# Issuing the last six stores of a batched matrix product as three pieces each

## The chip, the cores and the metric

The kernel runs on one core of one Trainium2 chip. The metric is the device time of one execution in microseconds (us), given as the median of several runs. The profile is one execution recorded by the hardware profiler; its span runs from the first to the last instruction.

## What is computed

```python
a, b: float32, shape (1024, 64, 64)
out = np.matmul(a, b)          # 1024 products of 64 x 64 matrices, float32
```

Inputs are 16.8 MB each, and so is the output: 33.55 MB are read from HBM and 16.78 MB written.

## The kernel before

The batch is cut into 16 tiles of 64 matrices, `t` = 0 to 15 (`n_t` = 16), for `b` and for the output, and into 8 tiles of 128 matrices for `a`.

For each output tile, VectorE casts `b` to bfloat16 (`cast`), VectorE copies the transposed `a` into a block-diagonal tile (`spread`), TensorE multiplies (`multiply`, line 189), and ScalarE, with some help of VectorE, copies the product from PSUM into the tile `o_sb` in SBUF (`evacuate`, line 177). `a` was regrouped by VectorE and transposed by TensorE before that. The loop over `t` is written out by hand under a manual schedule: in each step the next tile's `spread` and `cast` come first, then the loads of tiles further ahead, then this tile's `multiply`, and then the store of the tile before it (`HOLD` = 2, so that `store(t - 1)` follows `multiply(t)`).

`o_sb` has 128 partitions of 8 KB. In the output one partition holds, for each of the eight groups of matrices `gh`, one run of 1 KB. A store of `n` groups therefore writes `n` runs of 1 KB for each partition.

Stores are made by `put(lo, n)` in `multiply`, lines 165 to 169; `lo` is the first group and `n` the number of groups. Which queue issues them is decided by `store_queue` (lines 64 to 67):

- Tiles 0 to 13 are stored whole, 1 MB in one DMA, by GpSimd's queue.
- Tile 14 is stored in two halves of 512 KB (`lo` = 0 and 4), both by the queue of SyncE (SP).
- Tile 15 is stored in four quarters of 256 KB (`lo` = 0, 2, 4, 6). Quarters 0 and 2 (`lo` = 0 and 4) are issued by ScalarE's queue (ACT) and quarters 1 and 3 by SP. ScalarE evacuates quarters 0 and 2, VectorE quarters 1 and 3.

So the last six stores are: the two halves of tile 14, called A and B below, and the four quarters of tile 15, called C (ACT), D (SP), E (ACT) and F (SP). SP issues A, B, D, F in this order, and ACT issues C, E. Nothing else is left on SP's instruction list behind F but the wait for the end (line 282, the launch), where SP waits for every completion semaphore in turn before the engines are released.

The framework gives each DMA that SP or ACT issues one of eight completion semaphores, in turn. A DMA adds 16 to its semaphore when all of it has landed. Before a semaphore is used again, the issuing queue waits until the DMA that had it before has landed. Such a wait stands in the issuing engine's instruction list, directly ahead of the DMA or in it. In this kernel the six last stores have six of the eight semaphores, and the ones that had them before were loads.

Of the kernel before, what the change touches and what calls it, by code (L numbers as in the profile page):

```python
# [13 lines left out]
def kernel(  # L14
# [19 lines left out]
    n_t, n_s = B // 64, B // 128  # L34
# [7 lines left out]
    o_v = out.rearrange("(t gh x) (mo w) n -> t (x mo) gh (w n)", gh=8, x=8, w=4)  # L42
# [21 lines left out]
    def store_queue(t, lo):  # L64
        if t < n_t - 2:
            return nc.gpsimd
        return nc.scalar if t == n_t - 1 and lo % 4 == 0 else nc.sync
# [90 lines left out]
    def multiply(t):  # L158
        at_bd = bd_tiles[t % N_BD][:].rearrange("p j g wl h mo -> p j g (wl h mo)")
        at_bd = at_bd.bitcast(bf16).rearrange("p j g (c u) -> p j g c u", u=2)  # L160
        b_bf = bbf_tiles.pop(t)
        last = t == n_t - 1
        o_sb = o_pool.tile([128, 8, 2, 2, 64], fp32, name="o_sb")

        def put(lo, n):
            store_queue(t, lo).dma_start(  # L166
                out=o_v[t, :, lo : lo + n, :],
                in_=o_sb[:, lo : lo + n].rearrange("p gh j wl n -> p (gh j wl n)"),
            )

        def evacuate(o_ps, gh, n, copies):

            for par in range(2):
                for wl in range(2):
                    src = o_ps[64 * wl : 64 * wl + 64, :, par, :, :]
                    dst = o_sb[64 * par : 64 * par + 64, gh : gh + n, :, wl, :]
                    copies[2 * par + wl](dst, src)  # L177

        for half in range(2):
            if not last:  # L180
                o_ps = o_psum.tile([128, 4, 2, 2, 64], fp32, name="o_ps")
            for g8 in range(8):
                if last and g8 % 4 == 0:
                    o_ps = t_psum.tile([128, 2, 2, 2, 64], fp32, name="at_ps")
                g = 8 * half + g8
                gl = (g8 % 4 if last else g8) // 2
                for j in range(2):
                    for u in range(2):
                        nc.tensor.matmul(  # L189
                            o_ps[:, gl, g % 2, j, :],  # L190
                            at_bd[:, j, g, :, u],
                            b_bf[:, g, 64 * u : 64 * u + 64],
                            start=(u == 0),
                            stop=(u == 1),
                        )
                if last and g8 % 4 == 3:
                    copy = nc.scalar.copy if g8 == 3 else nc.vector.tensor_copy
                    evacuate(o_ps, g // 4 * 2, 2, [copy] * 4)
            if not last:
                copies = [nc.scalar.copy] * 4  # L200
                if half and t % 2:
                    copies[2:] = [nc.vector.tensor_copy] * 2
                evacuate(o_ps, 4 * half, 4, copies)
        if last:
            held[t] = [lambda q=q: put(2 * q, 2) for q in range(4)]
        else:
            whole = t < n_t - 2
            held[t] = [lambda q=q: put(q, 8 if whole else 4) for q in ([0] if whole else [0, 4])]
# [78 lines left out]
```

## Time and profile before

| What | Value |
|---|---|
| Median of 3 runs (134.76 to 134.84) | 134.77 us |
| Span of the profiled execution | 133.1 us |
| What lies around the span, against the median | 1.7 us |
| VectorE busy | 94.5 us (71%) |
| ScalarE busy | 87.8 us (66%) |
| TensorE busy | 65.7 us (49%) |
| Moved by the DMA engines | 45.01 MB, 338 GB/s on average |

The span is that of the one recorded execution, and no time of its own is recorded beside the span; the runs' median is 1.7 us longer, and this is taken for what lies around the span. "PE" is TensorE, "DVE" VectorE, "ACT" ScalarE, "POOL" GpSimd and "SP" SyncE; a "q" behind a name (SPq, ACTq) is the engine's sequencer, which issues DMAs and waits. The core has 16 DMA engines, and all queues share them. "DMA share" is the mean busy share of the sixteen; it can go a little above 1, since neighbouring packets overlap. "Landing" is the moment at which a DMA's completion semaphore has its full count.

### The profile page before, as it was taken

The page shows a single profiled execution, that of the slowest core. Times are in us where ns is not written, and L with a number is a line of the kernel's source. Part 1 is how long each engine was busy: PE and PEld are TensorE (multiplying, and loading weights), DVE is VectorE, ACT ScalarE, POOL GpSimd, SP SyncE. Part 2 cuts the span into 40 slices and gives each one's busy share as a digit, 9 for nine tenths or more (in the row PEclk, how much of TensorE's full clock was granted, in tenths as well). Part 3 has the DMA queues.
Part 4 walks back from the last instruction along what each step waited for, and adds up shares of the span by engine and source line. Part 5 has one row for each costly group of instructions (what it writes and reads, how often), then busy time and mean ns, then how long its engine had stood idle before and what let it go on. Part 6 is the DMA issues. An engine that isn't in the chain of part 4 may idle for free.

```text
span 133.1 us, 2837 instructions
## 1 busy us (share of the span) xinstructions
PE 65.7 (49%) x1152; PEld 62.7 (47%) x1152; DVE 94.5 (71%) x120; ACT 87.8 (66%) x161; POOL 33.7 (25%) x43
## 2 busy tenths in 40 slices
PE   0005504990068386059519672986199361776000
PEld 0005304980068275058509562975199360766000
DVE  5930299208999719598999699969999994978100
ACT  3134505899128999919899759696969987099600
POOL 8981000420082072143144022203020410210000
PEclk9999999999559999968996875579756985556855
DMA  3999999999999999999999999999999999999991
GB/s 75 367 332 311 307 312 279 278 307 326 328 307 402 316 322 334 393 385 401 318 282 365 402 397 356 308 307 387 395 396 387 393 396 391 402 403 402 380 339 41
DMA packets 19021, 45.01 MB, mean 338 GB/s; under 512 B 1088, under 2 KB 3136, under 8 KB 19008
## 3 DMA queue, kind: packets, MB, share of 16 engines
q0 software_dynamic: 6832, 20.19, 50.2%
q1 hardware_dynamic: 7120, 14.68, 30.5%
q10 hardware_dynamic: 5056, 9.96, 19.8%
q8 instruction: 9, 0.15, 0.4%
q14 instruction: 4, 0.03, 0.1%
HBM read 33.55 MB, written 16.78 MB: 378 GB/s over the span
## 4 chain that ended last, share of the span: by engine, by line
DMA 54%; DVE 18%; ACT 13%; issue 4%; PE 3%; SPq 1%; DVEq 0%; ACTq 0%
DMA b_sb<-in_b_dram 54%; ACT o_sb L177 9%; DVE at_bd L133 9%; DVE b_bf L144 4%; DVE o_sb L177 3%; PE at_ps L120 2%; ACT at_sb L123 2%; ACT b_bf L144 1%; PE o_ps L189 1%; DVE a_bf L108 1%; SPq L90 1%; DVE a_bf L111 1%; ACT b_bf L151 1%; SPq L96 0%; DVEq L133 0%
## 5 line engine op out<-in xcount | busy, mean ns | idle before, releaser
L177 ACT COPY o_sb<-o_ps 64x512 f32<-64x512 f32 x106 | 61.6, 581 | 9.5 <-PE o_ps L189 8.2
L189 PEld LDWEIGHTS <-at_bd 128*128 128x128 bf16 x1024 | 42.5, 113 | 39.7 <-DVE b_bf L144 26.8
L189 PE MATMUL o_ps<-b_bf,at_bd 128*128 128x64 bf16 x960 | 41.2, 213 | 36.0 <-DVE b_bf L144 25.1
L133 DVE COPY at_bd<-at_sb 32x1024 f32<-32x1024 f32 x64 | 46.6, 728 | 13.6 <-ACT at_sb L123 11.8
L120 PE MATMUL at_ps<-identity,a_bf 128*128 128x128 f32 x128 | 22.5, 350 | 19.3 <-ACT a_bf L105 11.4
L166 POOL DMA_DIRECT2D out_dram<-o_sb x14 | 16.3, 1166 | 55.4 <-ACT at_sb L123 23.0
L120 PEld LDWEIGHTS at_ps<-identity,a_bf 128*128 128x128 f32 x128 | 20.7, 190 | 19.4 <-issue 19.4
L144 DVE CAST b_bf<-b_sb 128x2048 bf16<-128x2048 f32 x14 | 17.5, 1249 | 10.0 <-DMA b_sb<-in_b_dram 9.8
L123 ACT COPY at_sb<-at_ps 128x512 f32<-128x512 f32 x32 | 17.4, 590 | 9.9 <-PE at_ps L120 7.6
L73 POOL DMA_DIRECT2D a_sb<-in_a_dram x21 | 13.3, 650 | 27.3 <-DVE a_bf L108 20.4
L177 DVE COPY o_sb<-o_ps 64x512 f32<-64x512 f32 x14 | 9.7, 690 | 0.3
L108 DVE COPY a_bf<-a_sb 128x3072 bf16<-128x3072 bf16 x7 | 7.4, 1059 | 0.0
L105 ACT CAST a_bf<-o_sb 128x1024 bf16<-128x1024 f32 x2 | 2.1, 1044 | 5.3 <-DMA o_sb<-in_a_dram 5.3
L111 DVE CAST a_bf<-a_raw 128x1024 bf16<-128x1024 f32 x7 | 4.8, 683 | 0.0
L144 ACT CAST b_bf<-b_sb 128x2048 bf16<-128x2048 f32 x1 | 1.9, 1897 | 4.1 <-DMA b_sb<-in_b_dram 4.1
L177 DVE COPY o_sb<-at_ps 64x256 f32<-64x256 f32 x8 | 3.4, 422 | 1.3 <-PE at_ps L189 1.2
L105 DVE CAST a_bf<-o_sb 128x1024 bf16<-128x1024 f32 x2 | 2.6, 1296 | 2.4 <-DMA o_sb<-in_a_dram 2.3
L189 PE MATMUL at_ps<-b_bf,at_bd 128*128 128x64 bf16 x64 | 3.6, 242 | 1.0 <-DVE at_bd L133 1.0
L217 DVE MEMSET at_bd<- 128x4096 f32 x1 | 3.5, 3472 | 0.8 <-issue 0.8
L151 ACT CAST b_bf<-b_sb 128x512 bf16<-128x512 f32 x2 | 1.1, 615 | 4.3 <-DMA b_sb<-in_b_dram 4.3
L177 ACT COPY o_sb<-at_ps 64x256 f32<-64x256 f32 x8 | 2.9, 367 | 0.1
L214 ACT ACT_TABLE_LOAD x1 | 1.3, 1283 | 2.3 <-issue 2.3
(12 smaller groups left out, 6.1 us busy)
## 6 DMA issues: line engine op xcount, KB each, us to landing
out_dram<-o_sb POOLq DMA_DIRECT2D x14, 1024.0 KB, 22.3
a_sb<-in_a_dram POOLq DMA_DIRECT2D x21, 256.0 KB, 16.4
a_raw<-in_a_dram SPq DMA_DIRECT2D x7, 512.0 KB, 19.1
o_sb<-in_a_dram SPq DMA_DIRECT2D x2, 512.0 KB, 6.2
o_sb<-in_a_dram ACTq DMA_DIRECT2D x2, 512.0 KB, 7.3
out_dram<-o_sb SPq DMA_DIRECT2D x2, 512.0 KB, 7.4
out_dram<-o_sb SPq DMA_DIRECT2D x2, 256.0 KB, 7.7
out_dram<-o_sb ACTq DMA_DIRECT2D x2, 256.0 KB, 5.9
```

The costliest lines, as they stand in the source:

```text
L73: nc.gpsimd.dma_start(out=a_sb[:, h, :, :].rearrange("p v k -> p (v k)"), in_=a_v[s, h])
L105: copy(a_bf[:, :, h, :], a_sb[h].rearrange("p (v k) -> p v k", v=16))
L108: nc.vector.tensor_copy(a_bf[:, :, 0:3, :], cast_sb[:].rearrange("p h v k -> p v h k"))
L111: nc.vector.tensor_copy(a_bf[:, :, 3, :], raw[:])
L120: nc.tensor.transpose(at_ps[:, vo, :], a_cols[:, 4 * vo + 2 * j + wl, :], identity[:])
L123: nc.scalar.copy(at_tiles[s][:, j, :, wl, :, :], at_ps[:].rearrange("p vo (g mp) -> p g mp vo", mp=4),)
L133: nc.vector.tensor_copy(bd[rows, :, :, :, h, :].rearrange("p j g wl mo -> p j (g wl) mo"), at_tiles[t // 2][rows, :, half, :, :, :].rearrange(
L144: (nc.vector.tensor_copy if t else nc.scalar.copy)(b_bf[:], b_sb[:])
L166: store_queue(t, lo).dma_start(out=o_v[t, :, lo : lo + n, :], in_=o_sb[:, lo : lo + n].rearrange("p gh j wl n -> p (gh j wl n)"),)
L177: copies[2 * par + wl](dst, src)
L189: nc.tensor.matmul(o_ps[:, gl, g % 2, j, :], at_bd[:, j, g, :, u], b_bf[:, g, 64 * u : 64 * u + 64], start=(u == 0), stop=(u == 1),)
L217: nc.vector.memset(bd_tiles[0][:], 0.0)
```

## The change

`put` is given a second form for the last two tiles. Where it made one DMA over 128 partitions, it makes three: over partitions 0 to 111, over the next 16 - r, and over the last r. r is 1 for A, 2 for B, 5 for C, 3 for D, 7 for E and 4 for F. All three are issued by the queue that issued the whole store, one after the other. Six DMAs become eighteen: twelve on SP and six on ACT. The bytes, the engines' computing and the stores of the first 14 tiles are as they were.

```diff
         def put(lo, n):
+            if t >= n_t - 2:
+                few = (1, 2)[lo // 4] if t == n_t - 2 else (5, 3, 7, 4)[lo // 2]
+                for first, end in ((0, 112), (112, 128 - few), (128 - few, 128)):
+                    store_queue(t, lo).dma_start(
+                        out=o_v[t, first:end, lo : lo + n, :],
+                        in_=o_sb[first:end, lo : lo + n].rearrange(
+                            "p gh j wl n -> p (gh j wl n)"
+                        ),
+                    )
+                return
             store_queue(t, lo).dma_start(
                 out=o_v[t, :, lo : lo + n, :],
                 in_=o_sb[:, lo : lo + n].rearrange("p gh j wl n -> p (gh j wl n)"),
```

The pieces of a store are called by its letter and a number: A1 is A's piece of 112 partitions, A2 that of 15 and A3 that of 1.

## Prediction

> **What bounds the end now.** I read the page's chain first (section 4): it follows the loads of `b` and ends at ScalarE's last copy, so it doesn't show the stores. Then, because the change touches nothing before 120 us, I read only the last 13 us. The timeline of the tail shows when the six stores are issued:
>
> ```profile
> 119.48 2.96 ACT L177 COPY o_sb<-o_ps 64x512 f32<-64x512 f32 x5
> ...
> 120.08 5.45 SPq L166 DMA_DIRECT2D out_dram<-o_sb  x4
> 120.30 3.49 DVE L177 COPY o_sb<-at_ps 64x256 f32<-64x256 f32 x8 [1.19 <-PE at_ps L189]
> 122.46 1.89 ACT L177 COPY o_sb<-at_ps 64x256 f32<-64x256 f32 x5
> 123.99 0.40 ACTq L166 DMA_DIRECT2D out_dram<-o_sb  x1
> 124.37 1.12 ACT L177 COPY o_sb<-at_ps 64x256 f32<-64x256 f32 x3
> 125.52 0.38 ACTq L166 DMA_DIRECT2D out_dram<-o_sb  x1
> ```
>
> Computing is over at 125.5. The windows of the tail (columns: stretch, its length, busy time of PE, PEld, DVE, ACT, POOL, the granted clock, DMA share, GB/s) show what remains:
>
> ```profile
> 126.00:127.00 1.00, 0.00 (x0) 0.00 (x0) 0.00 (x0) 0.00 (x0) 0.00 (x0) 0.50 1.07 374
> 127.00:128.00 1.00, 0.00 (x0) 0.00 (x0) 0.00 (x0) 0.00 (x0) 0.00 (x0) 0.50 1.09 378
> 128.00:129.00 1.00, 0.00 (x0) 0.00 (x0) 0.00 (x0) 0.00 (x0) 0.00 (x0) 0.50 1.04 361
> 129.00:130.00 1.00, 0.00 (x0) 0.00 (x0) 0.00 (x0) 0.00 (x0) 0.00 (x0) 0.50 0.66 230
> 130.00:131.00 1.00, 0.00 (x0) 0.00 (x0) 0.00 (x0) 0.00 (x0) 0.00 (x0) 0.50 0.23 81
> 131.00:132.00 1.00, 0.00 (x0) 0.00 (x0) 0.00 (x0) 0.00 (x0) 0.00 (x0) 0.50 0.03 10
> ```
>
> The sixteen DMA engines are full until 129 and then end one by one. All is queued long before: the end is set by draining. 378 GB/s over 16 engines is 1 KB per 43 ns on each. SP's waits close it:
>
> ```profile
> SPq L282 <- DMA out_dram<-o_sb: 6.1, 1, 6.1
> SPq L166 <- DVE o_sb L177: 0.9, 1, 0.9
> ```
>
> SP waits 6.1 us at line 282 for stores. The answers for line 166, asked store by store, give the price of an issue and the time to landing. B first, then D and F, on SP:
>
> ```profile
> L166 SPq DMA_DIRECT2D out_dram<-o_sb x1: 377/377/377, 122.5 to 122.5; - x1
> ...
> DMA to landing us min/median/max: 7.3/7.3/7.3
> ...
> L166 SPq DMA_DIRECT2D out_dram<-o_sb x2: 1227/1250/1274, 122.9 to 124.3; - x2
> ...
> DMA to landing us min/median/max: 7.5/7.7/8.0
> ```
>
> With the trace's records of the semaphores, A lands at 127.72, B at 129.72, C at 129.96, D at 130.90, E at 131.26 and F at 131.76. F is last; from there to the end of the span are 1.35 us of closing waits.
>
> **What the change removes, adds and moves.** Computing, the loads and the first 14 stores stay; their cover is complete, since nothing after them is issued differently before 120.48 (A1's issue in place of A's). The bytes stay too. What is added are twelve DMAs, and what matters is which semaphore each has. The built program's list has eighteen stores on eight completion semaphores, so ten of them must wait for an earlier piece to land:
>
> ```
> B2 waits for A1    E2 for A2    E3 for A3
> B3 waits for C1    D1 for C2    D2 for B1    D3 for C3
> F1 waits for E1    F2 for B2    F3 for E2
> ```
>
> SP's order is A1 A2 A3 B1 B2 B3 D1 D2 D3 F1 F2 F3. A wait holds everything behind it on its queue: B2's and B3's hold all of D and F, though VectorE has D's data ready at 122.0 and F's at 123.8. Before, none of the six waited for a store. ACT's E2 and E3 wait too; nothing but the closing drain is behind them.
>
> Step 1, when B3 gets free. It needs C1 landed. C landed at 129.96. In front of its end on the last DMA engine, A and B are shorter by 4 KB each (112 rows over 16 engines are 7 rows of 4 KB instead of 8) and C itself by 2 KB: 10 KB x 43 ns = 0.43 us. C1 lands at about 129.5. Bounds: not later than 129.96, since nothing is put in front of it but A2 and A3, which are no more than what A1 lost; not sooner than A1's 127.55 and its own 14 KB, 128.15. I take 129.5, since B1 shares the engines with it as B did with C. D1 and D2 need C2 and B1, which land by then: B1 at 129.72 - 0.34 (8 KB) = 129.4.
>
> Step 2, the issues behind it. B3, D1, D2, D3, F1, F2, F3: six issues stand ahead of F3. The price of one is 0.38 to 0.40 (A, B, C, E) and 0.05 to the next: 0.44 x 6 = 2.64 us, so F3 is issued at 132.15. The dear rows are D and F, 1.27 and 1.23: both followed another store on their queue by under 0.1 us, 0.85 us over the others. After the change D2 and F2 follow D1 and F1 at once in the same way. Bounds for the two: nothing, or 2 x 0.85 = 1.7 us. I take 0.5, nearer to the cheap rows: the engines are nearly idle by then (DMA share 0.23 in 130 to 131), and D1 and F1 have 224 runs where B had 512. F3 is issued at 132.65. E1 lands before 131.26, while F1 asks for it at about 131.5; F2's and F3's other waits (B2, issued at 127.6, and E2, at 127.5) are over by 131 as well.
>
> Step 3, from F3's issue to its landing. No row shows a small store on empty engines. From the first load's issue (0.74) to the first packet in the trace (2.16) are 1.42 us, and from the last packet's end (131.44) to F's landing 0.32 us; 2 KB per engine are 0.09 us: 1.83. The other bound is the shortest issue to landing in the whole trace, 4.5 us, of a 512 KB load beside three others. I take 2.0, near the sum of parts. F3 lands at 134.65.
>
> Sum: 134.65 - 131.76 = +2.89. The closing waits run through the semaphores 60 ns apart; F3's stands four places later than F's did, so that much less follows: -0.24. Together +2.65 on the span of 133.1, that is 135.75; with the 1.7 around it, or 134.77 + 2.65, 137.4 us.
>
> [...] What the trace shows of the engines is that they end far apart: the sixteen completions of F run from 128.61 to 131.76, so bytes moved from the last engine to an early one would be worth time. [...]
>
> **Rivals.** *The drain is relieved and the waits don't count* (faster). The last engine ends alone: its last packet at 131.44, the next engine's at 130.86. If the pieces take one row of each store off the last engine, 16 KB x 43 ns = 0.69 us go, of which the next engine allows 0.58: 134.2 us. For it: the spread of the completions. Against it: F3 would have to be issued by 131.18 - 2.0 = 129.2, and so C1 to land by about 126.5, when the windows show the engines still full and A itself not landed. It decides only if the waits end 3 us sooner than I have them. Chance 2%.
>
> *The short chain* (slower by less). C1 lands at its lower bound, D2 is then held by B1 at 129.4, and F3 follows four issues later: 129.4 + 1.76 = 131.16, landing 1.83 later at 133.0, +1.23 - 0.24 = +1.0: 135.8 us. For it: D and F no longer compete with C for the engines. Against: in the drain the two queues share the engines, as B and C landed 0.24 us apart. Chance 17%.
>
> *The dear issue* (slower by more). D2 and F2 cost the full 0.85 each: 1.2 us over the forecast, and with C1 at 129.96 another 0.46: 138.6 to 139.1 us. For it: both SP stores that followed another closely paid it. Against: they were issued into full engines. Chance 28%.
>
> *Nothing happens*, since the drain hides the pieces: 134.8 us. It would need F3's landing at 131.8, as far from the waits as the first rival. Chance 1%.
>
> **How the numbers follow.** The forecast, 137.4, has 52%; the two neighbours on the slow side 17% and 28%. A range of 8 in 10 reaches into both of these and leaves out about the outer third of each (6 and 9%) and the 3% of the other cases: 136.0 to 138.9 us. A change of 0.2% (0.27 us) is about what can be told from none here. Slower by more than that: 52 + 17 + 28 = 97%; same 1%, faster 2%.
>
> **What would show it.** In the profile after: SP's waits list stores of line 169 waiting for `out_dram` DMAs, above all one of 4 to 5 us ahead of B2 (122.9 to about 127.5) and one of 1.5 to 2 us ahead of B3; F1's issue at 131 or later; a DMA share that falls off near 128.5 and comes back for D and F. F3 lands some 2 us after its issue, and the last SP wait at the launch line is short. The step fails if SP issues F before 130, or if small pieces take far more than 2 us to land.

## The result and the profile after

The changed kernel takes 136.07 us (median of four runs, 135.96 to 136.7) against 134.76 (134.71 to 134.84) for the kernel before on the same chip: a ratio of 1.0108 [1.0083, 1.0134], or +1.31 us. The recorded execution took 135.96 us with a span of 134.1; before, the span was 133.1.

The windows of the tail of the changed kernel, in the columns used above for the kernel before:

```profile
126.00:127.00 1.00, 0.00 (x0) 0.00 (x0) 0.00 (x0) 0.00 (x0) 0.00 (x0) 0.50 1.02 314
127.00:128.00 1.00, 0.00 (x0) 0.00 (x0) 0.00 (x0) 0.00 (x0) 0.00 (x0) 0.50 1.02 322
128.00:129.00 1.00, 0.00 (x0) 0.00 (x0) 0.00 (x0) 0.00 (x0) 0.00 (x0) 0.50 0.94 261
129.00:130.00 1.00, 0.00 (x0) 0.00 (x0) 0.00 (x0) 0.00 (x0) 0.00 (x0) 0.50 0.64 191
130.00:131.00 1.00, 0.00 (x0) 0.00 (x0) 0.00 (x0) 0.00 (x0) 0.00 (x0) 0.50 0.82 229
131.00:132.00 1.00, 0.00 (x0) 0.00 (x0) 0.00 (x0) 0.00 (x0) 0.00 (x0) 0.50 0.70 191
132.00:133.00 1.00, 0.00 (x0) 0.00 (x0) 0.00 (x0) 0.00 (x0) 0.00 (x0) 0.50 0.33 105
```

Two things are to be seen. The DMA share falls to 0.64 at 129 and comes back to 0.82 at 130, where before it went on down from 0.66 to 0.23: the engines run short of work while D and F are still to be issued. And between 126 and 128 the engines are as busy as before (1.02 against 1.07 to 1.09), yet they move 314 to 322 GB/s and not 374 to 378: they are busy, and do less.

SP's waits of the changed kernel (columns behind the colon: us in total, times, longest):

```profile
SPq L169 <- DMA out_dram<-o_sb: 3.9, 3, 2.7
SPq L292 <- DMA out_dram<-o_sb: 0.9, 1, 0.9
```

Stores now wait for stores, 3.9 us in three waits, and the last wait at the launch line has shrunk from 6.1 to 0.9 us. The timeline of the queues shows how long SP is at it:

```profile
120.32 11.33 SPq L169 DMA_DIRECT2D out_dram<-o_sb  x12
...
125.36 3.38 ACTq L169 DMA_DIRECT2D out_dram<-o_sb  x4
```

SP's issues, which ended at 125.5, now reach to 131.65. The trace's records of the single instructions and of the semaphores give the chain behind it (us):

| Piece on SP | Issued | Issue took | What held it |
|---|---|---|---|
| A1, A2, A3, B1 | 120.32, 120.75, 122.12, 123.57 | 0.37, 1.32, 1.34, 1.21 | nothing but the issue ahead |
| B2 | 127.47 | 0.33 | A1, landed 127.46 |
| B3 | 128.22 | 0.24 | C1, landed 128.20 |
| D1 | 129.30 | 0.32 | C2, landed 129.24 |
| D2, D3 | 129.67, 130.14 | 0.42, 0.29 | issue ahead (B1 had landed at 129.36) |
| F1, F2, F3 | 130.52, 130.89, 131.35 | 0.32, 0.42, 0.30 | issue ahead |

F3 lands last, at 132.99, where F landed at 131.76 before. The three holds are 2.69, 0.42 and 0.85 us, about the 3.9 of the waits. How the second sight, busy engines that move less, comes in is settled by the experiments.

The view of the DMA queues, cut to 119 to 134 us, shows it in one number (columns: queue, kind, packets, MB, share of the time of 16 engines). In the kernel before:

```profile
q1 hardware_dynamic: 1600, 1.57, 29.9%
```

The same view of the changed kernel:

```profile
q1 hardware_dynamic: 1667, 1.57, 35.4%
```

q1 is SP's queue. The same 1536 packets of 1 KB (A, B, D and F) take 29.9% x 15 us x 16 engines / 1536 = 47 ns each before and 55 ns after. Over all six stores, 2048 packets, the trace's records give a mean of 46.4 ns before, with 0.5% of them over 60 ns, and 54.3 ns after, with 16.2%. Per engine, 128 packets are 5.9 us before and 7.0 after. These means serve below as the measure of **slow packets**. They come from one recorded execution of each kernel, the times from the median of several.

### The profile page after: what moved, and what is told of

Its sections match the earlier page's. It is cut to its first block, busy times and chain, and to the rows that moved or that the text cites. A ratio compares the mean times of both kernels' runs of the same rounds, so it can differ in the third digit from the quotient of the medians.

```text
span 134.1 us, 2850 instructions
## 1 busy us (share of the span) xinstructions
PE 63.4 (47%) x1152; PEld 60.0 (45%) x1152; DVE 93.4 (70%) x120; ACT 87.8 (65%) x161; POOL 33.6 (25%) x43
## 4 chain that ended last, share of the span: by engine, by line
DMA 53%; DVE 14%; ACT 14%; PE 5%; issue 5%; SPq 1%; ACTq 0%; DVEq 0%
DMA b_sb<-in_b_dram 53%; ACT o_sb L187 10%; DVE at_bd L133 6%; DVE b_bf L144 4%; DVE o_sb L187 3%; PE o_ps L199 3%; ACT at_sb L123 2%; PE at_ps L120 2%; ACT b_bf L144 1%; SPq L90 1%; DVE a_bf L108 1%; ACT b_bf L151 1%; DVE a_bf L111 0%; SPq L96 0%; ACTq L169 0%
## 5 line engine op out<-in xcount | busy, mean ns | idle before, releaser
L199 PEld LDWEIGHTS <-at_bd 128*128 128x128 bf16 x1024 | 41.9, 112 | 42.6 <-DVE b_bf L144 27.8
L133 DVE COPY at_bd<-at_sb 32x1024 f32<-32x1024 f32 x64 | 46.6, 728 | 13.9 <-ACT at_sb L123 11.2
L176 POOL DMA_DIRECT2D out_dram<-o_sb x14 | 16.2, 1154 | 57.7 <-ACT at_sb L123 21.8
L120 PE MATMUL at_ps<-identity,a_bf 128*128 128x128 f32 x128 | 20.6, 329 | 19.0 <-DVE a_bf L105 10.7
L120 PEld LDWEIGHTS at_ps<-identity,a_bf 128*128 128x128 f32 x128 | 18.7, 175 | 19.0 <-issue 19.0
L108 DVE COPY a_bf<-a_sb 128x3072 bf16<-128x3072 bf16 x7 | 6.7, 951 | 0.0
L105 DVE CAST a_bf<-o_sb 128x1024 bf16<-128x1024 f32 x2 | 1.6, 781 | 3.9 <-DMA o_sb<-in_a_dram 3.9
```

Of the source, the lines that this page charges most:

```text
L105: copy(a_bf[:, :, h, :], a_sb[h].rearrange("p (v k) -> p v k", v=16))
L108: nc.vector.tensor_copy(a_bf[:, :, 0:3, :], cast_sb[:].rearrange("p h v k -> p v h k"))
L120: nc.tensor.transpose(at_ps[:, vo, :], a_cols[:, 4 * vo + 2 * j + wl, :], identity[:])
L133: nc.vector.tensor_copy(bd[rows, :, :, :, h, :].rearrange("p j g wl mo -> p j (g wl) mo"), at_tiles[t // 2][rows, :, half, :, :, :].rearrange(
L176: store_queue(t, lo).dma_start(out=o_v[t, :, lo : lo + n, :], in_=o_sb[:, lo : lo + n].rearrange("p gh j wl n -> p (gh j wl n)"),)
L199: nc.tensor.matmul(o_ps[:, gl, g % 2, j, :], at_bd[:, j, g, :, u], b_bf[:, g, 64 * u : 64 * u + 64], start=(u == 0), stop=(u == 1),)
```

## The experiments

All kernels below differ from the kernel before in `put` (and, where it is said, in `held`). `before` was run again beside each group. First theory: the waits on SP set the end. Rivals: the number of DMAs, the uneven load of the engines, or the pieces themselves cost the time. The indented paragraphs are the expectations, written before the kernels ran.

### One store in three, all six in equal thirds, all six in two

`f_three` cuts F alone; its pieces have the issues but no wait for a store. `even_three` and `two_pieces` cut all six, with the same loop (each kernel has one of the three lines with `cuts`):

```diff
+            if t >= n_t - 2:
+                cuts = (0, 112, 124, 128) if t == n_t - 1 and lo == 6 else (0, 128)  # f_three
+                cuts = (0, 48, 96, 128)                                              # even_three
+                cuts = (0, 112, 128)                                                 # two_pieces
+                for first, end in zip(cuts, cuts[1:]):
+                    store_queue(t, lo).dma_start(out=o_v[t, first:end, ...], in_=o_sb[first:end, ...])
+                return
```

`f_three`:

> Only F (the last quarter) is cut, into 112, 12 and 4 partitions: eight DMAs for eight semaphores, so that no piece waits for a store. Theory 'waits' (the loss of the change comes from SP standing at semaphores that earlier pieces still hold): 134.8 us, within 0.2 of before; F's pieces are issued from 124.3 on, some 1.3 us apart, by 128 at the latest, and the end stays that of the drain. Rival 'pieces' (small DMAs cost time by themselves, by their issue or by their rows on few engines): part of the 1.3 us shows here, 135.0 to 135.4 us, with F's third piece the last to land. [...]

Measured: 134.82 against 134.81, 1.0003 [0.9989, 1.0017]. Two more DMAs at the very end of SP's list cost nothing that can be told, and the piece of four partitions is not dear by itself.

`even_three`:

> Each of the six stores is cut into 48, 48 and 32 partitions: eighteen DMAs as in the change, each of them on all sixteen engines with equal rows. The semaphores are handed out anew; SP's last wait chain is F1 for C3, F2 for E1, F3 for B3. Theory 'waits': still slower than before, 135.3 to 136.1 us, F3 issued between 130 and 131 (the pieces that are waited for are smaller and land a little sooner than those of 112). Rival 'pieces' by uneven rows: 134.8 us, as before.

Measured: 136.09 against 134.81, 1.0104 [1.0066, 1.0142]. Here every piece brings sixteen completions, as a whole store does (SP's 1728 packets between 119 and 134 us are 1536 of 1 KB and 12 x 16 completions), and the loss is that of the change, at the upper end of what theory 'waits' had. Uneven pieces (16 - r and r) are not needed for it. B3 is held until 127.97, D1 until 128.79 (C1's landing), and F3 lands at 132.98. The packets take 54.9 ns.

`two_pieces`:

> Each of the six stores is cut into 112 and 16 partitions: twelve DMAs, four of which wait (D1 for A1, D2 for A2, F1 for B1, F2 for C1), all on sixteen engines. Theory 'waits': what is waited for lands by 127.5 (A) and 128.2 to 129.4 (C, B), so F1 is issued at about 129.4 and F2 at 129.9, and F2 lands near 131.6, where the drain of before ended: 134.6 to 135.1 us. Rival 'pieces', in proportion to the added DMAs (six of twelve): 135.4 us.

Measured: 135.24 against 134.81, 1.0043 [1.002, 1.0067]. With twelve DMAs only four of SP's must wait for a store. F1 is held for B1 until 129.44, and F2 lands last, at 132.44. It lies between the two expectations. Fewer waits, less loss; but the packets are slow here too, 53.6 ns, and F1 and F2 take 2.6 to 2.8 us to land. So this run doesn't tell a wait from a slow packet.

### Relieving one engine

`relieve15` cuts only A and B, into 120 and 8 partitions: `cuts = (0, 120, 128) if t == n_t - 2 else (0, 128)`. Eight DMAs have eight semaphores, so no store waits for another.

> A and B are cut into 120 partitions (fifteen engines by the count that divides, eight rows each) and 8 (eight engines, one row each); C to F are whole. Eight DMAs, no wait for a store. [...] If the engine that ends last is the sixteenth, 0.6 us are gained: 134.2 us. If it is one of the first eight, 8 KB at 43 ns a KB are lost: 135.1 us. If it is one of the others, nothing: 134.8 us. The landings after the change (A2, on fifteen engines, has the straggler of A1) say that it is not the sixteenth, so 134.8 to 135.1.

Measured: 136.03 against 134.81, 1.0092 [1.0062, 1.0122]. This was missed: +1.2 us without any wait. Stores cut by partitions can cost this much without them. The packets take 51.3 ns, 10.9% of them over 60. A second theory followed: stores cut by partitions are read more slowly, whatever waits there are. The slower packets are 128 x 4.9 ns = 0.63 us per engine, half of the loss. What makes up the rest is not shown; the load of the engines is uneven here (A's first piece brings fifteen completions, its second eight, and B's likewise: SP's 1614 packets between 119 and 134 us are 1536 of 1 KB and 78 completions, of which D and F have 32), and between 124 and 126 us they were not full (a DMA share of 0.86 and 270 GB/s, before 1.05 and 382). No record names an engine, so which one is the expectation's sixteenth, and which are its first eight, was not shown.

### Eight DMAs, no waits: partitions against columns

All three cut only A and B in two. `ab_112` and `ab_halves` cut the partitions; `ab_columns` cuts the groups, so that every piece still has 128 partitions:

```diff
+                cuts = (0, 112, 128) if t == n_t - 2 else (0, 128)   # ab_112
+                cuts = (0, 64, 128) if t == n_t - 2 else (0, 128)    # ab_halves
+                cuts = (0, 2, 4) if t == n_t - 2 else (0, 2)         # ab_columns: of the groups
+                    out=o_v[t, :, lo + first : lo + end, :],         # ab_columns
```

`ab_112`:

> A and B are cut into 112 and 16 partitions, C to F are whole: eight DMAs, no wait for a store, every engine has the same eight rows as before. Theory 'waits alone': 134.8 us. Theory 'slow packets' (a 1 KB packet of a store that isn't laid over all 128 partitions takes longer: 54.3 ns on average over the last six stores after the change, where before it was 46.4): the 64 packets that each engine has of A and B take some 8 to 10 ns more each, 0.5 to 0.65 us: 135.3 to 135.5 us.

`ab_halves`:

> A and B are cut into partitions 0 to 63 and 64 to 127, C to F are whole: eight DMAs, no wait for a store, equal rows on all engines. [...] Theory 'waits alone': 134.8 us.

`ab_columns`:

> A and B are cut by groups instead, into two pieces of 128 partitions and two groups each; C to F are whole: eight DMAs, no wait for a store. As many DMAs, bytes and runs as in the two other kernels of this kind, but the layout over the partitions stays. Both theories: 134.8 us, packets at 46 ns. If the mere cut of A and B in two costs, it shows here.

| Kernel | us, before 134.86 | Ratio | 1 KB packet, mean | over 60 ns |
|---|---|---|---|---|
| ab_112 | 135.66 | 1.0054 [1.0035, 1.0073] | 51.5 ns | 8.7% |
| ab_halves | 135.81 | 1.0069 [1.0045, 1.0093] | 51.5 ns | 10.5% |
| ab_columns | 134.83 | 0.9998 [0.9982, 1.0013] | 46.6 ns | 1.0% |

The same number of DMAs, the same bytes, no waits for stores: cut by partitions they lose 0.8 to 0.95 us, cut by columns nothing. The second theory stands, and the two added DMAs by themselves are out. One size was missed: `ab_112` lost more than the 0.5 to 0.65 us expected. The halves' packets are no slower than those of 112 and 16: with C to F at 46.4 ns, A's and B's took about 57 ns in both (an estimate from the means).

### Eighteen DMAs of 128 partitions

`columns18` keeps the change's eighteen DMAs and ten waits, but every piece has 128 partitions: A and B in two, one and one groups, the quarters in one group and two halves of a group's run.

```diff
...
+                if t == n_t - 2:
+                    cuts = [(lo + c, lo + d, 0, 256) for c, d in ((0, 2), (2, 3), (3, 4))]
+                else:
+                    cuts = [(lo, lo + 1, 0, 256), (lo + 1, lo + 2, 0, 128), (lo + 1, lo + 2, 128, 256)]
...                  (one DMA for each of the three)
```

> All six stores are cut into three pieces by groups and by half runs (A and B: two groups, one, one; C to F: one group, and the other one's 1 KB runs in two halves of 512 B): eighteen DMAs with ten waits for earlier stores, each over all 128 partitions. SP's last waits are F1 for B3, F2 for C1, F3 for C2. Theory 'waits': F1 at 129.6, F3 at 130.5 to 130.7, landing 1.6 to 1.8 us later at 132.2 to 132.5, 0.3 to 0.5 us behind the drain's end: 135.1 to 135.5 us, and packets of 1 KB at 46 ns. Theory 'slow packets alone': 134.8 us, unless the runs of 512 B cost something.

Measured: 135.07 against 134.86, 1.0019 [1.0007, 1.003], +0.2 us, just under the range expected; 1 KB packets 47.0 ns. Ten waits cost little here, though SP does stand at them, for half as long as in the change:

```profile
SPq L173 <- DMA out_dram<-o_sb: 1.9, 3, 1.3
```

The records say why: the pieces waited for are smaller and land sooner (A's first at 126.88, B's last at 129.21), so SP issues D's second piece at 126.90 and F's first at 129.28; the last piece lands at 132.00, 0.24 us after F before. So the count of waits doesn't set the loss; when the DMAs waited for land does. Nor are the 0.2 us all due to waits for certain: the 1024 packets of 512 B took 27.8 ns each, which is 0.3 us more per engine than 512 packets of 1 KB at 46.4.

### The waits without the pieces

`waits_only` keeps the six whole stores and issues, behind each, two tiny loads of 16 - r and r rows of 256 B into a scratch tile, so that eighteen DMAs share the eight semaphores while the stores keep their 128 partitions.

```diff
+                store_queue(t, lo).dma_start(<the whole store>)
+                for rows in (16 - few, few):
+                    c = 64 * tiny.pop()
+                    store_queue(t, lo).dma_start(out=scratch[0:rows, c : c + 64], in_=b[0, 0:rows, :])
+                return
```

> The six stores are whole again (128 partitions), and each is followed on its queue by two tiny loads (16 - r and r rows of 256 B from b into an unused tile) in place of the two small pieces: eighteen DMAs on the same semaphores in the same order as in the change, so the same queues wait for the same places, but the output leaves in whole stores. Theory 'waits': SP stands until B and C have landed (129.2 to 129.9), F is issued at about 130.3 to 130.8, and its second tiny load, which follows D's landing, at about 131.3 to 131.6, landing near 133: 135.6 to 136.1 us, as much as the change loses, with packets at 46 to 47 ns. Theory 'slow packets alone': 134.8 us.

Measured: 135.93 against 134.87, 1.0082 [1.0069, 1.0095], +1.06 us. The packets are not slow: 46.6 ns, 0.6% over 60. Unlike what was expected, its semaphores are dealt out a little otherwise than in the change: D waits for A, the first load behind D for B, the second for C, the first behind F for D. SP's waits in this kernel:

```profile
SPq L170 <- DMA out_dram<-o_sb: 1.8, 1, 1.8
SPq L176 <- DMA out_dram<-o_sb: 1.7, 1, 1.7
SPq L296 <- DMA out_dram<-o_sb: 0.7, 1, 0.7
```

and SP's timeline (the stores are line 170, the tiny loads line 176):

```profile
120.22 0.42 SPq L170 DMA_DIRECT2D out_dram<-o_sb  x1
...
127.74 0.41 SPq L170 DMA_DIRECT2D out_dram<-o_sb  x1
129.88 0.62 SPq L176 DMA_DIRECT2D scratch<-in_b_dram  x2
130.60 0.41 SPq L170 DMA_DIRECT2D out_dram<-o_sb  x1
131.05 0.76 SPq L176 DMA_DIRECT2D scratch<-in_b_dram  x2
```

D is held for 1.8 us and the load behind it for 1.7, to 129.88, when B has landed (129.87). F can't be issued before 130.60, and the last DMA lands at 133.03, practically where F3 does in the change (132.99). F itself, a whole store, lands at 132.76, 1.0 us later than before. So the waits, with the issues that queue up behind them, cost some 1.1 us without any slow packet.

### Halves by partitions, by columns, and the middle partitions

The last three test the second theory where it should be strongest: A, B and the two halves of tile 15 are each stored as two DMAs, eight in all, with no wait for a store. `halves8` reads partitions 0 to 63 and 64 to 127, `whole8` two groups each over 128 partitions, and `middle8` is `halves8` with both pieces read from partitions 32 to 95, written to the same output rows, so that its last two tiles are not the product.

```diff
-            held[t] = [lambda q=q: put(2 * q, 2) for q in range(4)]
+            held[t] = [lambda q=q: put(4 * q, 4) for q in range(2)]
...
+                for first, end in ((0, 64), (64, 128)):
+                    queue = nc.sync if t == n_t - 2 or first else nc.scalar
+                    queue.dma_start(out=o_v[t, first:end, lo : lo + n, :],
+                                    in_=o_sb[first:end, lo : lo + n]...)    # halves8
+                                    in_=o_sb[32:96, lo : lo + n]...)        # middle8
```

`halves8`:

> No semaphore is waited for twice, but every byte of the last two tiles leaves in a store that isn't over 128 partitions: A, B and the two halves of tile 15 (quarters 0 and 1 together, 2 and 3 together), each as partitions 0 to 63 and 64 to 127: eight DMAs of 256 KB. [...] Theory 'waits alone': 134.8 us, or a little more, since quarter 1 goes out 1.1 us later than before.

`whole8`:

> The control for the kernel of halves: the same four halves of 512 KB, each in two pieces by groups over all 128 partitions, eight DMAs of 256 KB, no wait for a store. Both theories: 134.8 us, packets at 46 to 47 ns.

`middle8`:

> As the eight halves of 64 rows, but both pieces of each store read partitions 32 to 95 of the tile in SBUF (the output of the last two tiles is therefore not the product), while they write the same rows of the output as there. Eight DMAs of 64 rows, four rows on each engine, no wait for a store. [...] Theory 'writes of the output' or 'count of rows' (the number or place of the rows written makes the packets slow, not where they are read): 51 ns or more on average and 135.5 us as in the halves.

| Kernel | us, and before | Ratio | 1 KB packet, mean | over 60 ns |
|---|---|---|---|---|
| halves8 | 135.55, 134.87 | 1.0058 [1.0037, 1.0079] | 52.6 ns | 17.1% |
| whole8 | 134.74, 134.87 | 0.9991 [0.9978, 1.0003] | 46.4 ns | 0.6% |
| middle8 | 134.96, 135.07 | 0.9996 [0.9981, 1.001] | 46.7 ns | 1.3% |

SP's line in the view of the DMA queues between 119 and 134 us, of `halves8`:

```profile
q1 hardware_dynamic: 1632, 1.57, 33.1%
```

of `whole8`:

```profile
q1 hardware_dynamic: 1632, 1.57, 30.0%
```

and of `middle8`:

```profile
q1 hardware_dynamic: 1632, 1.57, 30.2%
```

Same packets, same bytes; only the halves take more engine time. The window of `halves8` from 126 to 128 us shows the same as in the change, a full share with less moved:

```profile
126.00:128.00 2.00, 0.00 (x0) 0.00 (x0) 0.00 (x0) 0.00 (x0) 0.00 (x0) 0.50 1.03 305
```

The same window of `whole8`:

```profile
126.00:128.00 2.00, 0.00 (x0) 0.00 (x0) 0.00 (x0) 0.00 (x0) 0.00 (x0) 0.50 1.07 373
```

and of `middle8`:

```profile
126.00:128.00 2.00, 0.00 (x0) 0.00 (x0) 0.00 (x0) 0.00 (x0) 0.00 (x0) 0.50 1.06 367
```

In `middle8` the pieces have the 64 rows, the sizes, the queues and the output addresses of `halves8`, and it loses nothing. So for halves it isn't the number of rows, nor where the pieces are written; it is which partitions of SBUF a piece reads. (In `middle8` both pieces read the same bytes; no run separates that.) For pieces of 112, 15 or 1 partitions no such run was made.

The loss of `halves8`, 0.68 us, is no more than what A and B alone cost in `ab_112` and `ab_halves` (0.8 and 0.95 us), though twice the bytes are cut by partitions. It is near what its packets would give, 128 per engine x 6.2 ns = 0.79 us. But this is no proof that the packets alone are the way to the loss. The recorded execution, from which the 52.6 ns come, is the shortest of its eight: it took 134.92 us, no more than before, and its last store landed at 131.84, as F did before (131.76). So slow packets need not reach the end. In `middle8`, where packets are fast, one DMA engine ended well after the others (the last two completions of the last store are at 130.67 and 132.16); in `halves8` they lie close together (131.75 and 131.84).

What it is about the partitions that makes the difference was not shown. The runs give the mean of a 1 KB packet: 52.6 ns with pieces read from partitions 0 to 63 and 64 to 127, 46.4 with all 128 and 46.7 with 32 to 95; and 51.5, 51.3 and 54.9 with stores cut into 112 and 16, 120 and 8, and 48, 48 and 32 partitions.

### What the experiments say together

Two causes, each worth more than half of the loss without the other:

- SP's waits for reused semaphores, with the issues behind them: `waits_only`, +1.06 us with packets as fast as before.
- The partitions that a piece reads: `ab_112`, `ab_halves`, `halves8`, +0.7 to +0.95 us without any wait, all with slow packets; neither in their counterparts `ab_columns`, `whole8` and `middle8`.

How the second cause becomes lost time is not isolated. Beside the slow packets, SP began its last store later in these three kernels and in `relieve15` (126.2 to 127.8 us, in the counterparts 125.7 to 125.9), and the engines were less full between 124 and 126 us (a DMA share of 0.86 to 0.99 against 1.02 to 1.07).

The two don't add: 1.06 + 0.8 would be 1.9 us, and the change costs 1.31. In the changed kernel the end is reached through SP's chain of waits. The drain behind it is slower as well, but what doesn't hang on SP's waits is over well before the chain is (ACT's last piece, E3, lands at 130.62). Slow packets enter the chain only as far as they delay the landings that SP waits for, and those of the last pieces. The last hold ended with C2's landing at 129.24, sooner than the last hold in `waits_only`, which ended with B's at 129.87. How much of the 1.31 us each would leave if the other were gone in this very kernel was not measured: a form of it with the same pieces and no waits would need eighteen completion semaphores, and SP and ACT have eight. `f_three` loses nothing: its pieces wait for loads only. Its packets are slow as well where F is read (52.5 ns for those begun between 128 and 130 us, 48.5 over all); why this does not reach the end is not shown.

## Why the prediction was right, and where its numbers were off

The sign and the mechanism were right: SP holds D and F for stores to land, and the small last piece then ends the kernel. The time, 136.07, lies at the lower edge of the range, 1.3 us under the forecast of 137.4 and beside the rival called the short chain (135.8): on the span, 134.1, it is that rival's +1.0 to the tenth. (What lies around the span was 1.9 us in the recorded execution and not the 1.7 taken, and the median is 0.1 above that execution; these make the rest of the 1.31.) Both the place inside the range, by 0.07 us, and the hit of that rival are in part luck. The rival had D2 held by B1; instead C2 held D1, D2 went out 0.27 us later than the rival had it, and F3 landed 0.19 us sooner after its issue. The forecast's own three steps were all too long. Step by step:

- **Step 1, C1 lands at 129.5: 1.3 us late.** A1's landing was right (127.46 against 127.55 given), but C1 landed at 128.20, on the lower bound of 128.15. The reason taken for 129.5 was that B1 competes with C1 as B did with C. It didn't: A2, A3 and B1 were issued at 1.2 to 1.3 us each, so B1's issue ran from 123.57 to 124.78, where B's had begun at 122.46 and taken 0.38, and C1's (from 124.22, 0.37 us) was over before it; B1's first completion came at 128.03, when fifteen of C1's sixteen were there. That this is the reason is argued from the times, no run isolates it. The wait for C2, which the forecast had over by then, took 0.64 us of the gain back: D1 was issued at 129.30 against 129.94.
- **Step 2, the issues: 0.65 us too much.** From D1 to F3 are five issues; forecast 5 x 0.44 + 0.5 = 2.7 us, measured 2.05. D2 and F2 cost 0.42 each: the dear issue, at 28% the largest rival, did not come. Where it did come was the head of the tail, at A2, A3 and B1, and there it cost nothing, since B2 had to wait for A1 until 127.46 anyway. F1's wait for E1 was over (130.13), as forecast.
- **Step 3, F3's landing: 0.36 us too much.** 1.64 us after its issue, not 2.0, and less than the 1.83 of the sum of parts.
- **The closing waits** follow F3 by 1.1 us instead of 1.35: the -0.24 of the forecast.
- **What the sum did not have at all** are the slow packets. The forecast said that the bytes stay and priced them at 43 ns per KB for pieces as for whole stores. `halves8` and `ab_112`, where no store waits for a store, lose 0.7 to 0.8 us. In the total the error stayed unseen; that the chain of waits covers most of it is argued above, not measured.
- **The first rival's reason fell too.** With no wait in the way the relief of the last engine was to give 0.58 us; `relieve15` has no wait and lost 1.2, though its slow packets stand in the way of a clean test. That the pieces take a row of each store off the engine that ends last was the author's assumption; no run shows it. What the records show are counts of completions: A2's 15 rows bring fifteen at their landings, C2's 11 rows eleven. And the engine that ends last doesn't look like one that was relieved: A1's last completion is at 127.46 and A2's at 127.62, 0.16 us later, about the time of a 4 KB row (0.17 us at the 43 ns per KB of before), which reads as if that engine got one of A2's fifteen rows.
- Of the signs named ahead, the DMA share fell off and came back (0.64, then 0.82), and the launch line's wait was short (0.9). The wait ahead of B2 was 2.7 us and not 4 to 5, as the issues before it were dear; the one ahead of B3 was 0.4 and not 1.5 to 2, which is step 1's error again; F1 was issued at 130.5 and not at 131.

## What to carry to other kernels

Before a store is cut, count the DMAs in flight against the completion semaphores (eight here for SP's and ACT's): a DMA that gets a used one waits in its engine's list for the earlier DMA to land, and holds everything behind it; what that costs depends on when that one lands (at most 0.2 us in `columns18`, 1.1 in `waits_only`). If a transfer must be cut, cut it along the free dimension and leave each piece its 128 partitions: `ab_columns` and `whole8` cost nothing, the same bytes cut by partitions 0.7 to 0.95 us. A full DMA share does not say that the engines are at their best; look at the GB/s beside it (305 in `halves8` and 373 in `whole8`, both at a full share).

## What the runs showed of the hardware

- **An issue's price went by when it was made, not by its size.** The issues of line 169 on SP in the changed kernel (min, median and max in ns, first and last start in us):

```profile
L169 SPq DMA_DIRECT2D out_dram<-o_sb x12: 238/348/1340, 120.3 to 131.3; - x12
```

The dearest, 1.34 us, is A3 with four runs of 1 KB, issued at 122.1 right behind another DMA into full engines (a DMA share of 0.97 between 122 and 123 us); D2, right behind D1 when the share was 0.64 to 0.82, took 0.42. In `waits_only`, tiny loads of one and two rows took 1.0 us on SP at 122.1 and 124.9, and loads of three and four rows 0.27 and 0.29 us after 130.

- **A small store at the end landed 1.64 us after its issue** (F3, 8 KB, with F1 and F2 still under way and a DMA share of 0.70). No row of the kernel before showed that.
- **1 KB packets took 46 to 47 ns or 51 to 55 ns on average, by the partitions that the DMAs read** (48.5 where F alone was cut). The mean hides it: 91% of the packets took 46 ns or less before and still 79% in the change, while 0.5% took over 60 ns before and 16.2% in the change (9 to 17% in `relieve15`, `ab_112`, `ab_halves` and `halves8`).
